# First layer's norm weights spread over the partitions by TensorE, and the last query tile taken before the triangular solve

## Chip, cores, metric

One NeuronCore of a Trainium2 chip runs the whole program. The metric is device microseconds from start to end of one execution; runs of the same kernel mostly agree within 0.3%.

## What is computed

A decoder trunk of four residual layers on 256 tokens of width 1024, in float32: pooling mixer, gated DeltaNet, latent attention, pooling mixer again, then a final norm.

```python
def rmsnorm(x, g):
    y = x * rsqrt(mean(x * x, axis=-1) + EPS)
    return y * g                              # g: one weight per column

for i in range(4):
    h = rmsnorm(x, norm_g[i])                 # norm_g: (4, 1024)
    x = x + mixer[i % 3](h)                   # each mixer: input projection ... output projection
return rmsnorm(x, final_g)

# DeltaNet (layer 1), per chunk and head: a lower triangular system
L = where(strict, k_beta @ k.T * decay, 0)
sol = triangular_solve(eye + L, [v_beta, k_beta * exp(g)])
```

## The kernel before

Tokens lie on the 128 partitions in two tiles, t = 0 and 1 (`xs[t]`). Each projection streams weights from HBM: `weights` (L97) loads a piece into a `raw` tile with a DMA from SyncE (SP), ScalarE (ACT) makes a rounded copy `whi` (L117), and VectorE (DVE), or for a few pieces GpSimd (POOL), makes the rest `wlo` (L119). Activations are split the same way (`split_out`, L196 and L201), and every product takes three TensorE matmuls (L127 to L129 where channels lie on partitions, L168 where tokens do).

**The order of the work is not written by hand.** The kernel is traced in program order, and a planner, told so in `build` (L1261), fixes ahead of time the order in which each engine issues, from its own estimate of how long things take. It also packs the tiles into SBUF: a tile may be given bytes that an earlier tile has left, and its first writer then waits for that tile's last reader. All engines issue strictly in the order fixed. Where the program wants an order kept, it says `later(ins)` (issue behind `ins` on the same engine).

**The start.** `load_x(0)` loads the first token tile. 24 transposes of the identity (`WARM`, L270) keep TensorE at work. `LayerIn(0)` then loads the norm weights: `gain_tile` (L273) spreads one row of 1024 floats over all partitions by two broadcasting DMAs on SP's queue, 256 KB in SBUF each, with the first weight piece between them. `start(0)` (L1218) computes the sum of squares (L210, ACT), the power -0.5 (L297, POOL, `xr`), the product of x, `xr` and gain (L304, DVE, `h`), turns h with TensorE (L324) and splits it into `hTh` and `hTl`, the operands of the first matmuls. Two weight pieces are split ahead of that, two more behind it (`E0`, `E1`). `load_x(1)` and `start(1)` do the same for the second token tile, queued behind the last of these pieces on ACT and DVE; there, half of each product is begun on POOL (`begin`, L292) and finished by ACT (L309).

**The solve.** In `gdn_layer` the steps run as `g0 k0 d a0 g1 k1 a1 s q0 v0 v1 v2 q1 V3 i c3 g2 u0 u1 g3` (L560). `s` is `substitution` (L714): the triangle's diagonal blocks go to HBM and come back as one tile `Lb`, then 31 steps on POOL follow, each a product `pr` that reads `Lb` (L728) and a subtraction into `Tb` (L732). `Tb` goes back over HBM (L735, then four DMAs L739) into `T`. `q0` and `q1` are the two halves of the queries (`channels`, L661): a convolution (L634 ACT, L637 DVE) into `cv`, SiLU on ACT into the tile `kqT` (L671), transposes on TensorE (L677) and products with the keys (L690). `v0` to `V3` are the values (L784 to L791, tile `vR`). `i` is `inverses` (L801): it transposes T (L811, DVE) and starts with products of T (L820, TensorE), both queued by `later` behind the last matmul and the last `wlo` of `V3`. `g2` is a gate whose matmuls have line L168. Tiles of all these, 4 KB a partition each, come from one pool (`big`, L70).

```python
    def channels(dst, c0, hf, which):          # L661
        banks = project(...)
        dst.append(big("kqT", 4, S))           # L665: the tile that is written by SiLU
    def substitution():                        # L714
        ...
        Lb = big("Lb", B, B)[:M * Q]           # L722
```

Of the kernel before, what the change touches and what calls it, by code (L numbers as in the profile page):

```python
# [8 lines left out]
F32 = mybir.dt.float32  # L9
# [7 lines left out]
P = 128  # L17
# [25 lines left out]
def trunk(ctx: ExitStack, tc: tile.TileContext, x, positions, norm_g, pool_w_in, pool_w_grp,  # L43
# [3 lines left out]
    nc = tc.nc  # L47
    PSUM = bass.MemoryType.PSUM

    WARM = 24  # L50
    FREE = 4
    EARLY = 6
    E0 = 2
# [200 lines left out]
    def load_x(t):  # L254
        for c in range(2):
            sl = slice(c * CW, (c + 1) * CW)
            nc.sync.dma_start(out=xs[t][:, sl], in_=x[0, t * P:(t + 1) * P, sl])

    load_x(0)
    neghalf = const.tile([P, 2], F32, name="neghalf")  # L260
    nc.gpsimd.memset(neghalf, -0.5)
    half = const.tile([P, 1], F32, name="half")
# [5 lines left out]
    nc.scalar.activation(warm, neghalf, AF.Silu)  # L268
    ps = bank(tps, "tp")
    for _ in range(WARM):  # L270
        nc.tensor.transpose(ps[:, :P], ident, ident)

    def gain_tile(row, between):  # L273
        g = gp.tile([P, D], F32, tag="gain", name="gain")
        for c in range(2):
            sl = slice(c * CW, (c + 1) * CW)
            nc.sync.dma_start(out=g[:, sl], in_=row[:, sl].to_broadcast([P, CW]))
            if c == 0 and between:
                between()
        return g  # L280

    class Normed:

        def __init__(self, row, between=None):
            self.g, self.early = gain_tile(row, between), {}

        def begin(self, t, a):
            sl = slice(a, a + CUT)  # L290
# [4 lines left out]
        def rest(self, t):  # L295
            r = small("xr", 1)
            mark["pool"] = nc.gpsimd.tensor_tensor(out=r, in0=ms[t], in1=neghalf[:, :1],  # L297
                                                   op=ALU.pow).ins
            hs = []
            for a in range(0, D, CW):  # L300
                h = wh.tile([P, CW], F32, tag="h", name="h")
                cut = CUT if (t, a) in self.early else 0
                sl = slice(a + cut, a + CW)
                nc.vector.scalar_tensor_tensor(out=h[:, cut:], in0=xs[t][:, sl], scalar=r[:, 0:1],  # L304
                                               in1=self.g[:, sl], op0=ALU.mult, op1=ALU.mult)
                hs.append(h)
                if not cut:
                    continue
                mark["rest"] = nc.scalar.activation(h[:, :CUT], self.early.pop((t, a)), AF.Copy,  # L309
                                                    scale=r[:, 0:1]).ins  # L310
            return hs

    class LayerIn(Normed):


        def __init__(self, i, between=None):
            super().__init__(norm_g[i:i + 1, :], between)
            self.hT = Split("hT", KD)

        def feed(self, t):  # L320
# [215 lines left out]
    def gdn_layer(i, j, hT):  # L536
# [121 lines left out]
        def power(o, a):  # L658
            nc.gpsimd.tensor_tensor(out=o, in0=a, in1=half, op=ALU.pow)

        def channels(dst, c0, hf, which):  # L661

            banks = project(cols_of(w_in, c0 + hf * CW), units(KD), hT, chan=True,
                            pool=() if which else (0, 4))
            dst.append(big("kqT", 4, S))  # L665
            for b in range(2):
                cv = [worka("cv", S) for _ in range(2)]
                conv(*[(banks[b][:, c * S:(c + 1) * S], (c0 + hf * CW) // P + 2 * b + c, cv[c])
                       for c in range(2)])
                for c in range(2):  # L670
                    nc.scalar.activation(dst[hf][:, 2 * b + c, :], cv[c], AF.Silu)  # L671
            for c in range(0, 4, 2):
                ps = bank(tps, "tp").rearrange("p (t a s) -> p t a s", a=2, t=NT)
                h = 4 * hf + c
                for a in range(2):
                    for t in range(NT):
                        nc.tensor.transpose(ps[:, t, a, :], dst[hf][:, c + a, t * P:(t + 1) * P],  # L677
                                            ident)
                sq = worka("sq", NT, 2, P)
                nc.scalar.activation(sq, ps, AF.Square)  # L680
                nc.vector.tensor_reduce(ssq[:, which, :, h:h + 2], sq, axis=AX.X, op=ALU.add)
                if which == 0:
                    nc.vector.tensor_copy(ktok[:, h:h + 2, :], ps[:, 0])
# [29 lines left out]

        def substitution():  # L714

            d_l = dram.tile([M * Q, B * B], F32, name="d_l")
            lv = d_l.rearrange("(t m d) (r c) -> t d r m c", t=NT, d=Q, r=B)
            for t in range(NT):
                for d in range(Q):
                    nc.sync.dma_start(out=lv[t, d],  # L720
                                      in_=LT[t][d * B:(d + 1) * B, :, d * B:(d + 1) * B])
            Lb = big("Lb", B, B)[:M * Q]  # L722
            nc.sync.dma_start(out=Lb, in_=d_l.rearrange("m (r c) -> m r c", r=B))
            pr = small("pr", 256, bufs=1)[:M * Q]
            for r in range(B - 1):
                n, c = B - 1 - r, r + 1
                pv = pr[:, :n * c].rearrange("m (a b) -> m a b", a=n)
                nc.gpsimd.tensor_tensor(out=pv, op=ALU.mult,  # L728
                                        in0=Lb[:, r, r + 1:, None].to_broadcast([M * Q, n, c]),
                                        in1=Tb[:, r:r + 1, :c].to_broadcast([M * Q, n, c]))  # L730
                tv = Tb[:, r + 1:, :c]
                mark["blocks"] = nc.gpsimd.tensor_tensor(out=tv, in0=tv, in1=pv,  # L732
                                                         op=ALU.subtract).ins
            d_t = dram.tile([M * Q, B * B], F32, name="d_t")
            nc.gpsimd.dma_start(out=d_t.rearrange("m (r c) -> m r c", r=B), in_=Tb)  # L735
            tv = d_t.rearrange("(m d) (r c) -> d r m c", d=Q, r=B)
            for d in range(Q):
                dd = slice(d * B, (d + 1) * B)
                nc.gpsimd.dma_start(out=Ts[dd, :, :, dd].rearrange("p t h c -> p (t h) c"),  # L739
                                    in_=tv[d])  # L740
            nc.vector.reciprocal(rki, rk)
            nc.vector.tensor_tensor(out=kds, in0=rk[:, 0, :], in1=DT[0][:, :, P - 1],
                                    op=ALU.mult)
            nc.vector.tensor_scalar(neG, eG[:, 1, :], -1.0, None, ALU.mult)
            nc.gpsimd.tensor_tensor(out=ktok, in0=ktok, op=ALU.mult,
                                    in1=kds[:, :, None].to_broadcast([P, H, P]))
# [470 lines left out]

    def start(t):  # L1218
        with later(*held_back["after"], *[mark[e] for e in ("act", "dve") if t]):
            for a in range(0, D, CW):  # L1220
                part_done(t, a, CW, apart=True)
            for a in range(0, D, CW):
                if t:
                    nxt.begin(t, a)
            nxt.feed(t)

    held_back["free"] = 100
    nxt = LayerIn(0, lambda: prefetch(0, (0,)))
    for k in range(1, E0):
        prefetch(k)  # L1230
    start(0)
# [40 lines left out]
```

## Time and profile before

| | |
|---|---|
| three runs | 859.98, 860.16, 857.79 us; median 859.98 |
| profiled execution | 860.12 us; its span 858.3 us (1.8 us lie outside) |
| TensorE (PE) busy | 836.9 us, 98% of the span |
| DVE, ACT, POOL busy | 69%, 57%, 18% |
| DMA | 140.4 MB, 164 GB/s over the span |

A row of the timeline gives start, duration, engine, line, operation, output<-inputs; in brackets how long that engine (PE matmuls, PEld weight loads) sat idle before it and what released it. Busy PE is not PE at its best pace: at half clock it is busy too.

### The profile page before, as it was taken

The numbers are of one execution on the slowest core, as the hardware profiler recorded it, in microseconds if no ns is written. First come the engines' busy times: TensorE is split into PE (matmuls) and PEld (weight loads), VectorE is DVE, ScalarE is ACT, GpSimd is POOL, SyncE is SP. The second block draws the span as 40 slices with busy tenths as digits, with TensorE's granted clock in tenths as the row PEclk, the third lists the DMA queues.
The fourth block names the chain that finished last, engine by engine and source line by source line (L and its number), as shares of the span: only waits on it lengthen the run. The fifth ranks groups of instructions, "written<-read, shape, count | busy, mean of one in ns | idle before, by whom it ended". The sixth has DMA issues, their size and how long they took to land.

```text
span 858.3 us, 16132 instructions
## 1 busy us (share of the span) xinstructions
PE 836.9 (98%) x5967; PEld 778.9 (91%) x5967; DVE 594.2 (69%) x1140; ACT 490.2 (57%) x1007; POOL 155.2 (18%) x295
## 2 busy tenths in 40 slices
PE   6999999999999989999999999999999999999996
PEld 5999998988999988788979998999989989999986
DVE  4689866556988976355577659678767668867852
ACT  5566564467855744355465654566555475555642
POOL 4000000233237980022212002000000210000012
PEclk8999999999999999899999999999999999999999
DMA  6766666646655554123547676743552546556551
GB/s 196 245 190 185 179 194 198 194 138 198 193 141 168 171 149 131 66 67 106 173 139 217 198 171 172 195 127 97 172 163 82 175 148 209 182 179 196 190 201 50
DMA packets 109239, 140.42 MB, mean 164 GB/s; under 512 B 21228, under 2 KB 51112, under 8 KB 109160
## 3 DMA queue, kind: packets, MB, share of 16 engines
q1 hardware_dynamic: 106800, 137.65, 53.1%
q0 software_dynamic: 528, 1.58, 0.7%
q8 instruction: 47, 0.77, 0.4%
q10 hardware_dynamic: 1832, 0.16, 0.2%
q14 instruction: 32, 0.26, 0.1%
HBM read 137.79 MB, written 1.58 MB: 162 GB/s over the span
## 4 chain that ended last, share of the span: by engine, by line
PE 82%; POOL 7%; DVE 5%; DMA 3%; issue 2%; ACT 1%; SPq 0%; POOLq 0%; ACTq 0%; DVEq 0%
PE acc L168 33%; PE acc L128 11%; PE acc L127 11%; PE acc L129 11%; POOL Tb L732 3%; POOL pr L728 2%; PE aux L127 2%; PE aux L128 2%; PE aux L129 2%; DVE wlo L119 1%; DMA gain<-in_norm_g_dram 1%; DVE cv L637 1%; DVE h L304 1%; PE aux L861 1%; DMA Gb<-d_g 1%
## 5 line engine op out<-in xcount | busy, mean ns | idle before, releaser
L119 DVE TENSOR_TENSOR wlo<-raw,whi 128x512 fp32r<-128x512 f32 (+1 forms) x493 | 342.5, 717 | 162.6 <-ACT whi L117 155.4
L117 ACT CAST whi<-raw 128x512 fp32r<-128x512 f32 (+1 forms) x508 | 301.8, 617 | 256.7 <-PE acc L168 100.4
L127 PE MATMUL acc<-hTh,whi 128*128 128x256 f32 x832 | 234.3, 282 | 1.2 <-DVE vc L637 1.2
L128 PE MATMUL acc<-hTl,whi 128*128 128x256 f32 x832 | 235.0, 283 | 0.0
L129 PE MATMUL acc<-hTh,wlo 128*128 128x256 f32 x832 | 233.8, 281 | 0.0
L127 PEld LDWEIGHTS acc<-hTh,whi 128*128 128x128 f32 x832 | 156.9, 189 | 1.8 <-DVE vc L637 1.4
L128 PEld LDWEIGHTS acc<-hTl,whi 128*128 128x128 f32 x832 | 156.9, 189 | 0.4
L129 PEld LDWEIGHTS acc<-hTh,wlo 128*128 128x128 f32 x832 | 156.8, 189 | 0.2
L168 PE MATMUL acc<-wlo,yTh 128*128 128x256 f32 (+1 forms) x384 | 116.5, 319 | 0.0
L168 PE MATMUL acc<-whi,yTh 128*128 128x256 f32 (+1 forms) x384 | 116.4, 323 | 0.0
L168 PE MATMUL acc<-whi,yTl 128*128 128x256 f32 (+1 forms) x384 | 92.7, 322 | 0.0
L168 PEld LDWEIGHTS acc<-wlo,yTh 128*128 128x128 f32 x384 | 72.1, 188 | 5.1
L168 PEld LDWEIGHTS acc<-whi,yTh 128*128 128x128 f32 x384 | 71.7, 188 | 5.2
L168 PEld LDWEIGHTS acc<-whi,yTl 128*128 128x128 f32 x384 | 63.2, 188 | 5.5
L292 POOL TENSOR_TENSOR hg<-x,gain 128x256 f32<-128x256 f32 x18 | 14.9, 834 | 259.1 <-DVE x L354 257.4
L168 PE MATMUL acc<-wlo,hTh 128*128 128x512 f32 (+1 forms) x144 | 56.3, 396 | 0.4 <-DVE wlo L119 0.2
L168 PE MATMUL acc<-whi,hTh 128*128 128x512 f32 (+1 forms) x144 | 55.6, 394 | 0.7 <-ACT hTh L196 0.7
L168 PE MATMUL acc<-whi,hTl 128*128 128x512 f32 (+1 forms) x144 | 45.7, 389 | 0.0
L435 POOL COPY win<-u 128x4 f32<-128x4 f32 x8 | 2.8, 355 | 177.2 <-ACT u L429 177.2
L168 PEld LDWEIGHTS acc<-whi,hTh 128*128 128x128 f32 x144 | 27.5, 191 | 6.8 <-ACT hTh L196 1.7
L168 PEld LDWEIGHTS acc<-wlo,hTh 128*128 128x128 f32 x144 | 27.3, 190 | 6.8 <-DVE wlo L119 1.7
L168 PEld LDWEIGHTS acc<-whi,hTl 128*128 128x128 f32 x144 | 26.8, 190 | 5.5
(339 smaller groups left out, 1444.5 us busy)
## 6 DMA issues: line engine op xcount, KB each, us to landing
raw<-in_pool_w_in_dram SPq DMA_DIRECT2D x60, 512.0 KB, 4.5
raw<-in_gdn_w_in_dram SPq DMA_DIRECT2D x48, 512.0 KB, 3.9
raw<-in_pool_w_out_dram SPq DMA_DIRECT2D x32, 512.0 KB, 4.2
raw<-in_mla_w_in_dram SPq DMA_DIRECT2D x24, 512.0 KB, 4.6
raw<-in_mla_w_uq_dram SPq DMA_DIRECT2D x36, 256.0 KB, 3.4
raw<-in_pool_w_grp_dram SPq DMA_DIRECT2D x16, 512.0 KB, 4.1
raw<-in_gdn_w_out_dram SPq DMA_DIRECT2D x16, 512.0 KB, 3.7
raw<-in_mla_w_ukv_dram SPq DMA_DIRECT2D x32, 256.0 KB, 3.3
```

The costliest lines, as they stand in the source:

```text
L117: a = nc.scalar.copy(hi, v)
L119: b = e.tensor_tensor(out=lo, in0=v, in1=hi.bitcast(F32), op=ALU.subtract)
L127: nc.tensor.matmul(o, lhsT=lhs[0], rhs=rhs[0], start=start, stop=False)
L128: nc.tensor.matmul(o, lhsT=lhs[0], rhs=rhs[1], start=False, stop=False)
L129: return nc.tensor.matmul(o, lhsT=lhs[1], rhs=rhs[0], start=False, stop=stop)
L168: nc.tensor.matmul(o, lhsT=act(k, t * P, P)[x], rhs=parts[j][z][:, sl], start=k == first and x == z == 0, stop=k == last and x == 1)
L292: nc.gpsimd.tensor_tensor(out=self.early[t, a], in0=xs[t][:, sl], in1=self.g[:, sl], op=ALU.mult)
L304: nc.vector.scalar_tensor_tensor(out=h[:, cut:], in0=xs[t][:, sl], scalar=r[:, 0:1], in1=self.g[:, sl], op0=ALU.mult, op1=ALU.mult)
L637: nc.vector.scalar_tensor_tensor(out=o[:, d:], in0=ps[:, :S - d], scalar=tp(3 - d, c), in1=o[:, d:], op0=ALU.mult, op1=ALU.add)
L728: nc.gpsimd.tensor_tensor(out=pv, op=ALU.mult, in0=Lb[:, r, r + 1:, None].to_broadcast([M * Q, n, c]), in1=Tb[:, r:r + 1, :c].to_broadcast ...
L732: mark["blocks"] = nc.gpsimd.tensor_tensor(out=tv, in0=tv, in1=pv, op=ALU.subtract).ins
L861: nc.tensor.matmul(ps[:, c], lhsT=U[0][:, h, :], rhs=vR[h // 2][:, 0, c * DV:(c + 1) * DV], start=True, stop=True)
```

## The change

The first layer's norm weights are no longer spread by DMA. One row (4 KB) is loaded to one partition by a DMA on ACT's queue, ahead of everything else; two matmuls with a row of ones as the stationary operand write it to all partitions of two PSUM banks; they are pinned behind the warm-up transposes, of which there are 6 in place of 24. For the first token tile, DVE reads the weights from PSUM. For the second, ACT first copies both banks into an SBUF tile, since POOL reads them there. SP's queue loses the two broadcasts. The later layers load their norm weights as before.

In the DeltaNet layer, the tile of the second half of the queries is allocated at the head of `substitution`, with a one-column memset on POOL as its first write, so that its life overlaps that of `Lb` and it can't be given the same bytes. `channels` then uses that tile.

```diff
-    WARM = 24
+    WARM = 6
...
+    grow0 = const.tile([1, D], F32, name="grow0")
+    nc.scalar.dma_start(out=grow0, in_=norm_g[0:1, :])
     load_x(0)
+    ones = const.tile([1, P], F32, name="ones")
+    nc.gpsimd.memset(ones, 1.0)
...
     for _ in range(WARM):
-        nc.tensor.transpose(ps[:, :P], ident, ident)
+        tc.keep_in_program_order(nc.tensor.transpose(ps[:, :P], ident, ident))
+    gains0 = []
+    for c in range(2):
+        ps = bank(aux, "aux")
+        tc.keep_in_program_order(nc.tensor.matmul(ps, lhsT=ones, rhs=grow0[:, c * CW:(c + 1) * CW],
+                                                  start=True, stop=True))
+        gains0.append(ps)
...
-                                               in1=self.g[:, sl], op0=ALU.mult, op1=ALU.mult)
+                                               in1=self.g[:, sl] if self.g is not None else gains0[a // CW],
+                                               op0=ALU.mult, op1=ALU.mult)
...
+        taken = {}
+
+        def take(hf):
+
+            taken[hf] = big("kqT", 4, S)
+            nc.gpsimd.memset(taken[hf][:, 0, :1], 0.0)
...
-            dst.append(big("kqT", 4, S))
+            dst.append(taken[hf] if which and hf in taken else big("kqT", 4, S))
...
         def substitution():
 
+            take(1)
...
     def start(t):
         with later(*held_back["after"], *[mark[e] for e in ("act", "dve") if t]):
+            if t:
+                nxt.g = gp.tile([P, D], F32, tag="gain", name="gain")
+                for c in range(2):
+                    nc.scalar.copy(nxt.g[:, c * CW:(c + 1) * CW], gains0[c])
...
-    nxt = LayerIn(0, lambda: prefetch(0, (0,)))
+    nxt = LayerIn(0)
+    prefetch(0, (0,))
```

## Rows read from the trace of the kernel before

**Rows 1.** The page, part 4: engines' shares of the chain that ended last.
```profile
PE 82%; POOL 7%; DVE 5%; DMA 3%; issue 2%; ACT 1%; SPq 0%; POOLq 0%; ACTq 0%; DVEq 0%
```

**Rows 2.** PE's waits over the whole span: total us, times, longest us.
```profile
PE tp L324 <- DVE h L304: 4.4, 2, 2.4
PE tp L677 <- ACT kqT L671: 3.0, 3, 2.4
```

**Rows 3.** The timeline of the start, first token tile.
```profile
3.44 0.63 ACT L210 ACTIVATE junk<-x 128x512 f32<-128x512 f32 x1 [1.15 <-DMA x<-in_x_dram]
...
5.42 0.57 POOL L297 TENSOR_TENSOR xr<-ms,neghalf 128x1 f32<-128x1 f32 x1
...
7.83 0.75 DVE L304 SCALAR_TENSOR_TENSOR h<-x,xr,gain 128x512 f32<-128x512 f32 x1 [7.83 <-DMA gain<-in_norm_g_dram]
...
8.64 1.11 PE L324 MATMUL tp<-ident,h 128*128 128x128 f32 x4 [2.41 <-DVE h L304]
...
9.87 1.26 POOL L119 TENSOR_TENSOR wlo<-raw,whi 128x512 fp32r<-128x512 f32 x1 [3.88 <-ACT whi L117]
10.16 1.52 DVE L304 SCALAR_TENSOR_TENSOR h<-x,xr,gain 128x512 f32<-128x512 f32 x1 [1.57 <-DMA gain<-in_norm_g_dram]
...
11.74 1.11 PE L324 MATMUL tp<-ident,h 128*128 128x128 f32 x4 [1.99 <-DVE h L304]
```

**Rows 4.** The same timeline, second token tile and the weights between.
```profile
12.50 0.78 PE L168 MATMUL acc<-whi,hTh 128*128 128x512 f32 x1
...
12.81 1.43 POOL L292 TENSOR_TENSOR hg<-x,gain 128x256 f32<-128x256 f32 x2 [1.67 <-DMA x<-in_x_dram]
...
13.37 1.14 ACT L117 CAST whi<-raw 128x512 fp32r<-128x512 f32 x2
...
16.38 0.40 PE L168 MATMUL acc<-whi,hTl 128*128 128x512 f32 x1
...
17.48 1.09 PE L324 MATMUL tp<-ident,h 128*128 128x128 f32 x8 [0.70 <-ACT h L309]
```

**Rows 5.** Stages of the start: busy us by engine, PEclk granted, DMA share, GB/s.
```profile
6.00:7.00 1.00, 0.23 (x3) 0.00 (x0) 0.00 (x0) 0.00 (x0) 0.00 (x0) 1.00 0.73 205
...
9.00:10.00 1.00, 0.75 (x4) 0.35 (x2) 0.00 (x0) 0.62 (x1) 0.13 (x1) 0.50 1.03 395
```

**Rows 6.** DMA issues up to 30 us: count, KB each, median us to landing.
```profile
rows<-in_pool_scale_dram ACTq DMA_DIRECT2D x2, 8.0 KB, 4.6
```

**Rows 7.** Groups by line up to 60 us: busy, mean ns, idle before.
```profile
L429 ACT COPY u<-acc 128x512 f32<-128x512 f32 x2 | 1.2, 588 | 0.4 <-issue 0.4
```

**Rows 8.** The timeline around the end of the solve.
```profile
299.02 0.85 ACT L791 ACTIVATE vR<-tp,rki 128x256 f32<-128x256 f32 x2
...
305.29 0.42 ACT L671 ACTIVATE kqT<-cv 128x256 f32<-128x256 f32 x1 [3.46 <-POOL pr L728]
...
305.76 0.69 PE L677 MATMUL tp<-ident,kqT 128*128 128x128 f32 x2 [2.41 <-ACT kqT L671]
...
306.25 1.12 DVE L119 TENSOR_TENSOR wlo<-raw,whi 128x512 fp32r<-128x512 f32 x1 [2.25 <-ACT whi L117]
```

**Rows 9.** Stages after that wait, columns as in group 5.
```profile
306.00:308.00 2.00, 2.00 (x11) 2.00 (x11) 1.75 (x3) 1.71 (x5) 1.86 (x3) 0.50 0.32 124
308.00:310.00 2.00, 2.00 (x16) 2.00 (x16) 1.97 (x5) 1.07 (x3) 2.00 (x3) 0.82 0.62 131
318.00:348.00 30.00, 30.00 (x185) 25.14 (x184) 19.17 (x33) 12.66 (x24) 3.19 (x4) 1.00 0.44 141
```

**Rows 10.** The chain that ended last, 298 to 325 us: start, us, what.
```profile
310.47 0.45 PE aux L690 x4
...
315.38 3.03 PE acc L168 x13
```

**Rows 11.** The way of T: POOL's timeline, DVE's timeline, and line L820's instructions.
```profile
311.48 2.68 POOL L739 DMA_DIRECT2D T<-d_t  x4
...
318.75 2.37 DVE L811 STREAM_TRANSPOSE U<-T 128x1024 f32<-128x1024 f32 x2 [1.91 <-DMA T<-d_t]
...
L820 PE MATMUL aux<-T,LT x32: 275/275/283, 318.3 to 330.3; 128*128 128x64 f32 x32
```

More of the change, by code (lines that the diff above doesn't have):

```diff
@@ L270, in trunk, with gain_tile @@
     for _ in range(WARM):
-        nc.tensor.transpose(ps[:, :P], ident, ident)
-    def gain_tile(row, between):
+        tc.keep_in_program_order(nc.tensor.transpose(ps[:, :P], ident, ident))
[5 more added lines that the diff above has]
+        gains0.append(ps)
+    def gain_tile(row):
         g = gp.tile([P, D], F32, tag="gain", name="gain")
@@ L277, in gain_tile, with __init__ @@
             nc.sync.dma_start(out=g[:, sl], in_=row[:, sl].to_broadcast([P, CW]))
-            if c == 0 and between:
-                between()
         return g
     class Normed:
-        def __init__(self, row, between=None):
-            self.g, self.early = gain_tile(row, between), {}
+        def __init__(self, row):
+            self.g, self.early = None if row is None else gain_tile(row), {}
         def begin(self, t, a):
@@ L313, in trunk, with __init__ @@
     class LayerIn(Normed):
-        def __init__(self, i, between=None):
-            super().__init__(norm_g[i:i + 1, :], between)
+        def __init__(self, i):
+            super().__init__(norm_g[i:i + 1, :] if i else None)
             self.hT = Split("hT", KD)
```

## The prediction

> **What bounds the kernel now.** First the chain that ended last: TensorE holds 82% of it, POOL 7% and DMA 3% [rows 1]. So time is won only where TensorE stands still or runs at half clock, or where a POOL or DMA stretch holds it. Then TensorE's own waits, over the whole span [rows 2]: two of the largest are the ones that this change touches, 4.4 us for h of the first layer and 3.0 us for the queries' tile `kqT`. The timeline shows what lies behind each. At the start, `xr` is ready at 5.42 + 0.57 = 5.99, but the first h starts at 7.83 and the second at 10.16, both released by the broadcasting DMA of the norm weights [rows 3]. At the solve, ACT stands 3.46 us before its first write of `kqT`, released by POOL's L728, the product that reads `Lb`: the new tile has the old one's bytes. TensorE stands 2.41 us for it and DVE 2.25 us, since the weight casts are queued behind ACT's waiting instruction [rows 8]. After that TensorE has a clock of 0.50 for 2 us and a mean of 0.82 for two more [rows 9]: 2 x 0.50 + 2 x 0.18 = 1.4 us of work lost. That 1.4 is my price for one fall of the clock.
>
> **The start, step by step.** *The row.* The gain row's DMA goes first on ACT's queue, at about 0.8, where SP's first issue is now. Nothing in the trace is quite like it. The first half of x, 64 times as large and issued at the same moment, is in use at 3.44 [rows 3]; rows of 8 KB on the same queue took 4.6 us, with other DMAs under way [rows 6]. So it lands between 3.4 and 5.4; I take 3.4, the row of the same stretch. *The matmuls.* Two float32 products of 128 columns, four instructions, take 0.45 us at full clock [rows 10], so 512 columns take 0.9 and both 1.8: done at 5.2, behind r at 5.99, hence free; from 5.4 and at half clock they would end at 9.0. The 18 warm-ups removed lay before any real work and cost nothing. *h.* From 5.99: 0.75, then 0.75 more. The second now takes 1.52, beside a POOL product of two SBUF tiles (9.87 to 11.13) [rows 3]. The transposes of each are 1.11 at the clock of now [rows 3], so they run 6.8 to 7.9 and 7.9 to 9.0, against 12.85: 3.8 us earlier. The first weights also come earlier: 512 KB less at the 205 to 395 GB/s of these stages [rows 5] is 2.5 to 1.3 us.
>
> The Trainium skill says (GPSIMD Engine Reference, 8. Key points) that POOL shares SBUF interfaces with VectorE and that they contend when a VectorE instruction has two SBUF inputs. The trace agrees, 1.52 against 0.75 us. By that rule the new h, with one input from PSUM, escapes it; without the rule the second h would end at 8.3 and the step would give 3.4 instead of 3.8.
>
> *The second token tile* sets when TensorE runs on without a break. Its sums of squares are queued on ACT behind two casts that now end at 14.51 [rows 4]; these move by 3.8 to 10.7. The change puts two copies from PSUM ahead of or among the sums, 0.588 each [rows 7], 1.2 together. x's second tile is there at 12.81 [rows 4], after the change 1.3 to 2.5 earlier, 10.3 to 11.5, so it is no later than ACT by more than 0.8, and then the copies lie in that wait. The gain at the second transposes (17.48 now [rows 4]) is 3.8 - 1.2 = 2.6; the ends are 3.8 (copies hidden) and 0.8 (the row late, 2.0, less 1.2). *The gap.* The twelve matmuls of the first token tile end at 16.78 now and would end at 13.0; the transposes follow at 14.9, so TensorE stands 1.9 us where it stands 0.7 [rows 4]. Idle stretches of 2.41 us at the start and at the solve were followed by half clock [rows 3, 5, 8, 9]. 1.9 is shorter, and a fifth weight piece may fill part of it: I take half the price, 0.7, ends 0 and 1.4. **Start: 2.6 - 0.7 = 1.9 us faster**, ends 3.8 faster and 0.6 slower.
>
> **The solve, step by step.** The wait of `kqT` on `Lb` goes: 2.41 idle + 1.4 clock = 3.8 us for TensorE, or at least the 2.25 that DVE wins if DVE's convolutions and casts set the pace. The memset on POOL is one column and stands before the 31 steps; bytes are free there if the tile gets ones that have not been used for long, so nothing. *What is late next* is T. It depends on POOL alone: the 31 steps end where they did, POOL goes on without a pause to the four DMAs L739 at 311.48 to 314.16, and DVE stood 1.91 us for their landing until 318.75 [rows 11]. TensorE's first use, L820, runs at 318.3 without a wait [rows 11], which is no accident of slack: TensorE came there late by exactly the stall before. If it comes 2.3 to 3.8 us earlier, it waits there that long, and DVE waits with it, with the casts behind L811.
>
> Would the planner put other work in front? It has 13 matmuls L168 of the gate there already, 3.03 us [rows 10]. In its order, ACT's write of `kqT` stands ahead of a weight cast that could have run [rows 8]: a planner that counted on the 3.46 us would have cast first. So its estimate of POOL is too fast, the stall is not in its plan, and without the stall its plan stays what it is. T stays at 318.3, TensorE starts again there, and since the new gap of 2.3 to 3.8 is nearest to the 2.41 that brought half clock, I add 1.4; the end 0 stands for no fall. From 318 to 348 TensorE has hardly a break to absorb it [rows 9]. The Trainium skill (TensorE: Matmul & The Clock Gate, Part 1) holds that idleness throttles TensorE to half and activity releases it; the 0.50 after the wait agrees [rows 9]; by it the end 0 is unlikely. **Solve: 1.4 us slower**, ends 3.8 faster and 1.4 slower.
>
> **Sum.** 860.1 (the profiled execution, 0.1 above the median of 859.98) - 1.9 + 1.4 = **859.6**. Own range, with the start's ends and 0 to 1.4 for the solve: 856.5 to 862.
>
> **Rivals.**
> *1. The plan adapts.* L820 is put some 16 matmuls further back (3.8 us at 3.03 / 13 = 0.23), as filler is there until the end of the gates. For it: the plan is made anew for the new program. Against: see above. Then 860.1 - 1.9 - 3.8 = 854.4.
> *2. The place passes on (slower).* The tile taken early occupies bytes that another tile had, and a later one gets `Lb`'s. Between s and q1, six tiles are allocated; the last, the third values' `vR`, is written by ACT from 299.02 [rows 8]. If it is the one, ACT stands from there until 305.29: 6.3 us in place of 3.46, 2.8 more, with the convolutions and casts of the queries behind it, and TensorE passes L820 at 321. That is also how the change would not do what it says: it decides from the point where the wait is 3.46 + 1.9 = 5.4 us, that is, where the waiting write is queued before 299.9. With 1.9 from the start 861.0, with nothing from it 862.9. For it: bytes were short enough for one reuse. Against: inverses' tiles are later and may take them at no cost.
> *3. The row is late.* At 5.4 us, TensorE cold: the second half of h's weights at 9.0, its transposes at 10.9, 2.0 earlier than now; less 1.2 for the copies and 0.7 for the gap nothing remains: 860.1 - 0.1 + 1.4 = 861.4.
>
> **How the numbers follow.** A run of this kernel can tell 0.3%, 2.6 us, from no change. Forecast 0.50, of which 0.09 lies below 857.4 (no fall of the clock in either gap) and 0.03 above 862.6; rival 1 0.26, all faster; rival 2 0.13, of which 0.08 is slower by over 2.6, since the start then gives little; rival 3 0.11, of which 0.05. Faster 0.09 + 0.26 = 0.35, slower 0.03 + 0.08 + 0.05 = 0.16, the same 0.49. The range takes in rival 1 with its start between 1.3 and 2.6, so from 853.7, and rivals 2 and 3 to 862.7.
>
> **What the changed profile would show.** Right: no DMA of gain in the first 15 us; first h at about 6.0, second transposes from 7.9; the second token tile's transposes near 14.9, with a gap of about 1.9 before them; ACT's first `kqT` of the second half with no wait on L728; and in its place TensorE waiting at L820, DVE at L811 for `T<-d_t` by more than 1.91. Wrong, at the start: a gap on DVE until a matmul lands, or the copies ahead of sums that were ready. Wrong, at the solve: TensorE without a wait at L820 and more matmuls L168 before it (rival 1), or ACT waiting for L728 with another tile (rival 2).

## The result: slower, by the new wait at the inverses

| | median | runs, lowest to highest | profiled execution, its span |
|---|---|---|---|
| before | 858.86 us | 10, 857.79 to 860.65 | 860.12, 858.3 |
| after | 862.60 us | 10, 860.38 to 865.58 | 862.61, 860.9 |

The ratio is 1.0036, 95% interval 1.0021 to 1.0051: 3.1 us slower by the ratio (1.8 to 4.4), 3.7 by the medians. The time lies inside the range of the forecast, 853.7 to 862.7, but at its slow end, where the forecast had no change.

TensorE's waits over the whole span of the changed kernel (total us, times, longest; [rows 2] are those of before) tell most of it:

```profile
PE aux L838 <- DMA T<-d_t: 6.6, 1, 6.6
PE tp L694 <- ACT kqT L688: 2.9, 2, 2.5
...
PE tp L334 <- DVE h L313: 0.6, 1, 0.6
```

L838 is the old L820, the first product with the inverses; L694 is L677, L334 is L324. The wait for h has shrunk from 4.4 to 0.6. The one for the queries' tile behind the solve is gone: what stands here at L694 is another, at 260, behind weights that came late. A new wait of 6.6 us stands at the inverses.

**The start**, as in [rows 3, 4] (start, us, engine, line, form, idle before and its releaser):

```profile
3.57 3.78 PE L280 MATMUL aux<-grow,ones 1*128 1x512 f32 x4
6.01 0.75 DVE L313 SCALAR_TENSOR_TENSOR h<-x,xr,aux 128x512 f32<-128x512 f32 x1 [6.01 <-POOL xr L306]
7.10 1.17 DVE L119 TENSOR_TENSOR wlo<-raw,whi 128x512 fp32r<-128x512 f32 x1 [0.35 <-ACT whi L117]
8.20 0.73 DVE L313 SCALAR_TENSOR_TENSOR h<-x,xr,aux 128x512 f32<-128x512 f32 x1
8.99 1.11 PE L334 MATMUL tp<-ident,h 128*128 128x128 f32 x4 [0.60 <-DVE h L313]
9.76 0.77 PE L168 MATMUL acc<-whi,hTh 128*128 128x512 f32 x1
17.03 0.66 PE L334 MATMUL tp<-ident,h 128*128 128x128 f32 x4 [0.25 <-ACT h L319]
```

The first h starts at 6.01, released by r and not by a transfer. The two products that spread the row take 3.78 us. VectorE puts a weight's low part ahead of the second h, and the second transposes start at 8.99. TensorE stands hardly at all before the second token tile: the first weights' products fill the time.

**The end of the solve**, beside [rows 8, 11]:

```profile
299.61 0.47 ACT L688 ACTIVATE kqT<-cv 128x256 f32<-128x256 f32 x1
312.49 2.68 POOL L757 DMA_DIRECT2D T<-d_t  x4
316.75 0.62 ACT L117 CAST whi<-raw 128x512 fp32r<-128x512 f32 x1 [7.30 <-DMA raw<-in_gdn_w_in_dram]
318.90 3.65 PE L838 MATMUL aux<-T,LT 128*128 128x64 f32 x16 [6.59 <-DMA T<-d_t]
319.37 2.37 DVE L829 STREAM_TRANSPOSE U<-T 128x1024 f32<-128x1024 f32 x2 [9.50 <-DMA T<-d_t]
```

ACT's first write of the last queries comes at 299.61, without a wait (305.29 after 3.46 before). The four transfers of the inverses are issued 1.0 us later than in [rows 11], and TensorE and VectorE stand 6.59 and 9.50 us for their landing. Nothing fills the time on TensorE, since it issues strictly in its order and the products with the inverses are next in it. The weights for the products behind them were late as well: ACT stands 7.30 us for a raw weight, and SP's load of it waited 9.9 us for a weight's low part on POOL, L119, which is queued there behind the solve's work.

The stretches around that wait (us, then the busy time of TensorE, weight load, VectorE, ACT, POOL, the granted clock, DMA share, GB/s; [rows 9] before):

```profile
312.00:319.00 7.00, 0.41 (x3) 0.13 (x1) 0.00 (x0) 1.88 (x5) 6.81 (x12) 0.88 0.61 187
319.00:326.00 7.00, 7.00 (x25) 6.23 (x26) 6.63 (x12) 0.60 (x1) 1.83 (x3) 0.50 0.39 108
326.00:328.00 2.00, 2.00 (x7) 1.56 (x6) 1.64 (x5) 0.91 (x2) 0.00 (x0) 0.62 0.40 155
```

TensorE is at the lower of its two levels, 0.50, for the 7 us behind the wait, and at a mean of 0.62 for two more: 7 x 0.50 + 2 x 0.38 = 4.3 us of work lost. The kernel before lost 1.4 behind its 2.41.

### The profile page after: what moved, and what is told of

It reads as the page before. It is cut to its first block, busy times and chain, and to the rows that moved or that the text cites. A ratio compares the mean times of both kernels' runs of the same rounds, so it can differ in the third digit from the quotient of the medians.

```text
span 860.9 us, 16103 instructions
## 1 busy us (share of the span) xinstructions
PE 838.7 (97%) x5953; PEld 777.8 (90%) x5953; DVE 592.1 (69%) x1140; ACT 492.5 (57%) x1009; POOL 158.0 (18%) x297
## 4 chain that ended last, share of the span: by engine, by line
PE 85%; POOL 7%; DVE 2%; DMA 2%; ACT 2%; issue 1%; SPq 0%; POOLq 0%; ACTq 0%
PE acc L168 34%; PE acc L128 12%; PE acc L127 12%; PE acc L129 12%; POOL pr L746 3%; POOL Tb L750 2%; PE aux L127 2%; PE aux L128 2%; PE aux L129 2%; DVE h L313 1%; DMA T<-d_t 1%; PE aux L838 1%; PE tp L1202 1%; DMA Lb<-d_l 1%; PE aux L879 1%
## 5 line engine op out<-in xcount | busy, mean ns | idle before, releaser
L119 DVE TENSOR_TENSOR wlo<-raw,whi 128x512 fp32r<-128x512 f32 (+1 forms) x493 | 340.8, 713 | 165.3 <-ACT whi L117 162.1
L168 PE MATMUL acc<-whi,yTh 128*128 128x256 f32 (+1 forms) x384 | 116.5, 323 | 0.0
L168 PE MATMUL acc<-wlo,yTh 128*128 128x256 f32 (+1 forms) x384 | 116.4, 319 | 0.0
L168 PE MATMUL acc<-whi,yTl 128*128 128x256 f32 (+1 forms) x384 | 92.6, 321 | 0.0
L168 PEld LDWEIGHTS acc<-wlo,yTh 128*128 128x128 f32 x384 | 72.2, 188 | 5.1
L168 PEld LDWEIGHTS acc<-whi,yTh 128*128 128x128 f32 x384 | 71.7, 188 | 5.2
L168 PEld LDWEIGHTS acc<-whi,yTl 128*128 128x128 f32 x384 | 63.2, 188 | 5.6
L168 PE MATMUL acc<-wlo,hTh 128*128 128x512 f32 (+1 forms) x144 | 58.2, 407 | 0.6 <-DVE wlo L119 0.3
L168 PE MATMUL acc<-whi,hTh 128*128 128x512 f32 (+1 forms) x144 | 56.7, 400 | 0.7 <-ACT hTh L196 0.7
L168 PE MATMUL acc<-whi,hTl 128*128 128x512 f32 (+1 forms) x144 | 46.7, 397 | 0.0
L168 PEld LDWEIGHTS acc<-wlo,hTh 128*128 128x128 f32 x144 | 28.2, 196 | 7.8 <-DVE wlo L119 2.6
L168 PEld LDWEIGHTS acc<-whi,hTh 128*128 128x128 f32 x144 | 28.1, 195 | 6.7 <-ACT hTh L196 1.4
L168 PEld LDWEIGHTS acc<-whi,hTl 128*128 128x128 f32 x144 | 27.5, 195 | 5.6
```

The costliest lines, as they stand in the source:

```text
L119: b = e.tensor_tensor(out=lo, in0=v, in1=hi.bitcast(F32), op=ALU.subtract)
L168: nc.tensor.matmul(o, lhsT=act(k, t * P, P)[x], rhs=parts[j][z][:, sl], start=k == first and x == z == 0, stop=k == last and x == 1)
```

## The experiments

Ratios are against the kernel before, run on the same chip beside it, with a 95% interval. The theory that the first of them test: the way from the solve to the inverses (the stores of the triangle's diagonal blocks to HBM, called the band from here on, their load back as `Lb`, 31 steps on POOL, a store, four loads) sets the end of this stretch, so that a freed wait ahead of it only moves.

### The two parts apart

Start alone: the changed kernel without

```
-            take(1)
```

> The start's part alone: the row of gain spread by TensorE, the six warm-up transposes, the copies; the last queries' tile takes its place where it did before. Theory (T's way sets the end of the solve, and the freed wait on the queries' tile only moves the stall to the inverses): TensorE waits for the queries' silu and the band as before (about 3 us before the transposes of the queries), the inverses wait not at all or under 1 us, and the 2.4 us by which the changed kernel was ahead at the first band stay to the end, so about 2.4 us less than the kernel before (ratio 0.997, 0.995 to 0.999). Rival (the start's part itself is what costs, by its copies, by the half clock of its gain products or by a plan that comes out otherwise): no gain or slower, ratio 1.000 to 1.004.

Solve alone: the kernel before with `take`, its call, and

```
-            dst.append(big("kqT", 4, S))
+            dst.append(taken[hf] if which and hf in taken else big("kqT", 4, S))
```

> The solve's part alone: the kernel before with the last queries' tile taken ahead of the solve, the start unchanged. Theory: the wait on the queries' tile is gone, the inverses wait 3 to 6 us instead, TensorE is at half clock for some 7 us behind that wait in place of 2 to 3 us, and the run is 2 to 5 us longer than before (ratio 1.002 to 1.006). The steps of the solve on POOL take over 45 us if VectorE's casts beside them are what lengthens them, and 44.6 us as before if it was the start's shift that lengthened them. Rival (the start is to blame): same as before or faster by up to 3.8 us (ratio 0.9955 to 1.000).

| | median | ratio |
|---|---|---|
| start alone | 858.57 us | 0.9988 (0.9972 to 1.0003) |
| solve alone | 863.33 us | 1.0034 (1.0018 to 1.0050) |

TensorE's waits around the solve, start alone and then solve alone (timeline):

```profile
304.89 0.44 PE L694 MATMUL tp<-ident,kqT 128*128 128x128 f32 x2 [2.41 <-ACT kqT L688]
```

```profile
318.53 3.64 PE L828 MATMUL aux<-T,LT 128*128 128x64 f32 x16 [6.63 <-DMA T<-d_t]
```

So the solve's part is what costs: 2.9 us by its ratio, 1.5 to 4.3, with the same 6.6 us of wait. The start's part does not cost, but gives about 1 us, and its interval reaches zero. The two together make 1.9, inside the interval of the whole change (1.8 to 4.4). The start's 1 us is less than the 2.4 expected. Two things in the traces bear on it. First, the start of one execution is no fixed number. The solve-alone kernel has the start of the kernel before, in the same order on TensorE, and there the second transposes came at 10.22 and those of the second token tile at 16.16, against 11.74 and 17.48 [rows 3, 4]. The execution that the forecast rested on began 1.3 us late. The band's stores begin at 249.0 in the solve-alone execution and at 248.3 in the changed kernel: a lead of 0.7 us, where the late execution (250.7) shows 2.4. And since the solve alone waits 6.63 us too, with nothing of the start's change in it, most of the 2.4 within that wait comes from the late execution. Second, in the start-alone trace the band's stores begin 2.1 us earlier than before but the first step on POOL only 0.9 (rows of that line: form, count, shortest/median/longest ns, first and last start; before, then start alone):

```profile
L720 SPq DMA_DIRECT2D d_l<-LT x8: 340/449/640, 250.7 to 254.0; - x8
L728 POOL TENSOR_TENSOR pr<-Lb,Tb x31: 232/564/966, 261.0 to 305.0; 64x31 f32<-64x31 f32 x2, 64x60 f32<-64x60 f32 x2, 64x87 f32<-64x87 f32 x2, 64x112 f32<-64x112 f32 x2
```

```profile
L737 SPq DMA_DIRECT2D d_l<-LT x8: 340/448/1513, 248.6 to 253.3; - x8
L745 POOL TENSOR_TENSOR pr<-Lb,Tb x31: 233/566/968, 260.1 to 304.2; 64x31 f32<-64x31 f32 x2, 64x60 f32<-64x60 f32 x2, 64x87 f32<-64x87 f32 x2, 64x112 f32<-64x112 f32 x2
```

The eight issues take 4.7 us in place of 3.3, and the slowest of these stores lands after 3.5 us in place of 2.2. From 261 on the end of the stretch hangs on POOL, in the kernel before as well (its queries wait for POOL's last reading of `Lb`), so of a lead ahead of the solve only what reaches POOL survives.

### The clock behind the wait

```
+                ps = bank(tps, "tp")
+                for _ in range(56):
+                    tc.keep_in_program_order(nc.tensor.transpose(ps[:, :P], ident, ident))
                 with later(mark["strip"], mark["dve"]):
                     inverses()
```

> The changed kernel with 56 more transposes of the identity between the last row products before the inverses and the inverses; nothing uses them. They only fill TensorE's wait: the inverses start when they did, but TensorE was busy meanwhile. Theory (the half clock behind the wait costs about 4 us of its own): the stretch behind the inverses is at full clock, and the run is 3 to 4 us shorter than the changed kernel, about level with the kernel before (ratio to before 0.999 to 1.001). Rival 1 (the clock behind the wait costs little, the lateness of the inverses is all): same as the changed kernel (ratio 1.0036). Rival 2 (the added transposes are themselves late, at half clock or held up by their bank): longer than the changed kernel by up to 6 us.

862.63 us, ratio 1.0031 (1.0017 to 1.0045): level with the changed kernel, as rival 1 has it. Yet the trace does not bear rival 1 out:

```profile
318.58 1.97 PE L838 MATMUL aux<-T,LT 128*128 128x64 f32 x16 [1.63 <-DMA T<-d_t]
```

```profile
319.00:326.00 7.00, 6.97 (x37) 5.57 (x36) 6.63 (x13) 0.00 (x0) 0.40 (x2) 1.00 0.09 35
```

The clock is 1.00 behind the inverses, and the 16 products take 1.97 us in place of 3.65. But the planner made its order anew: between the first product with the inverses and the first with the state (L915, tile `st`, the step behind the inverses) there are now 98 row products L168, in the changed kernel 84. 13 of the 14 had stood ahead of the inverses. At 0.23 each [rows 10] the 14 are 3.3 us, done in the same 46 us. By this count the half clock had cost some 3 us, near the 4.3 that the windows give, and the experiment gave them away again by its order. That is counted from the trace and not shown by the total, on which the experiment is inconclusive.

### The inverses earlier

```
-                nc.gpsimd.dma_start(out=Ts[dd, :, :, dd].rearrange("p t h c -> p (t h) c"),
-                                    in_=tv[d])
+                mark["blocks"] = nc.gpsimd.dma_start(
+                    out=Ts[dd, :, :, dd].rearrange("p t h c -> p (t h) c"), in_=tv[d]).ins
```

`mark["blocks"]` is what POOL's work for the last queries is queued behind; so far it was the solve's last step.

> The changed kernel with POOL's work for the last queries queued behind the four transfers of the inverses to memory instead of between or ahead of them. Theory (the way of the inverses from the solve to TensorE sets the end): the inverses reach TensorE 1 to 2 us sooner, its wait for them is shorter by as much, and the run is 1 to 2 us shorter than the changed kernel (ratio to before 1.001 to 1.003), unless the queries that now come later are then waited for. Rival (the inverses are not what sets the end): no change against the changed kernel (1.0036).

858.42 us, ratio 0.9985 (0.9970 to 0.9999): 4.4 us shorter than the changed kernel by the two ratios, more than the 1 to 2 expected. POOL and TensorE:

```profile
305.75 0.64 POOL L753 DMA_DIRECT2D d_t<-Tb  x1 [0.29 <-POOL Tb L750]
309.07 2.01 POOL L757 DMA_DIRECT2D T<-d_t  x3 [2.68 <-DMA d_t<-Tb]
312.94 2.35 PE L838 MATMUL aux<-T,LT 128*128 128x64 f32 x16 [2.68 <-DMA T<-d_t]
```

The products with the inverses start at 312.94 in place of 318.90. Of the 6.0 us, 3.4 come from the issue (309.07 for 312.49), and only part of these from the queue's order: the last step on POOL ends at 305.46 in place of 307.32, 1.9 earlier, and from there to the issue it takes 3.6 us in place of 5.2. Three of the four transfers go ahead of POOL's work for the queries; the fourth, issued at 312.31, stands behind its first product. Most of the rest is the landing: 2.4 us for each of the four in place of 4.5 to 5.5. Raw weights move less at that time, which was not tested by itself as the cause: the DMA share around the landing is 0.36 (309 to 315), in the changed kernel 0.61 (312 to 319), and in the experiment before it, where the same four took 6.1 to 6.7, 0.77.

Is it the inverses' lateness that costs, or is POOL's new order a gain by itself? The same edit with the start's part alone (`take(1)` left out):

> The start's part alone, with the inverses' four transfers ahead of POOL's work for the last queries, and the queries' tile where it was before. Theory (as long as TensorE waits at the queries' tile, the inverses come in time and are not what is waited for): the inverses land some 3 us sooner and nothing comes of it, the run is level with the start's part alone (ratio to before 0.998 to 0.9995). Rival (the order on POOL's queue gives its gain by itself, whatever stands ahead): 3 to 4 us shorter than the start's part alone (ratio to before 0.994 to 0.996).

858.63 us, ratio 0.9987 (0.9972 to 1.0002): level with the start alone at 0.9988, where the inverses also were in time. TensorE's waits from 290 to 330:

```profile
PE tp L694 <- ACT kqT L688: 3.0, 1, 3.0
PE acc L127 <- DVE vc L647: 1.0, 1, 1.0
```

It waits for the queries' tile as before and for the inverses not at all. The theory holds on both sides: inverses that come earlier, by the order on POOL's queue and by shorter steps together, are worth 4 us where they are waited for, and nothing where the queries' tile is waited for ahead of them. It also prices the change itself: with the inverses ahead, taking the tile early (858.42) is worth no more than not taking it (858.63), a wait of 2.7 us at the inverses in place of one of 3.0 at the tile.

### Why the steps on POOL got longer

From the first step to the end of the last, the solve took 44.6 us before and in both kernels with the tile in its old place; 47.1 with the solve's part alone and 47.6 in the changed kernel. With the busy wait and with the inverses earlier, where the tile is early too, it took 45.5 and 45.7, so the tile's place alone does not make the 3 us. POOL's and VectorE's rows of the changed kernel, of the same moment:

```profile
265.46 0.50 POOL L750 TENSOR_TENSOR Tb<-Tb,pr 64x156 f32<-64x156 f32 x1
266.04 1.59 POOL L746 TENSOR_TENSOR pr<-Lb,Tb 64x175 f32<-64x175 f32 x1
```

```profile
265.21 0.87 DVE L647 SCALAR_TENSOR_TENSOR vc<-acc,tap,vc 128x255 f32<-128x255 f32 x2
266.00 1.28 DVE L119 TENSOR_TENSOR wlo<-raw,whi 128x512 fp32r<-128x512 f32 x2
```

A step of 64x175 that starts with a pair of casts (two inputs from SBUF) ends just after them, 1.59 us; beside the convolutions, which read PSUM, a step of 64x156 takes 0.50. In the experiment above (inverses earlier), where no cast is on VectorE at that moment, the same 64x175 takes 0.48. To test the size, the cast was given no input in the five stages beside the solve:

```
+                if mark.get("single") and e is nc.vector:
+                    b = e.memset(lo.bitcast(F32), 0.0)
+                else:
+                    b = e.tensor_tensor(out=lo, in0=v, in1=hi.bitcast(F32), op=ALU.subtract)
```

> The changed kernel with VectorE's subtraction that makes the low part of a weight (two inputs) replaced by a fill with zeros (no input) in the five stages beside the solve's steps on POOL; the low parts of those weights are left out of the sum. Theory A (POOL's steps are long because VectorE's work with two inputs runs against them): the 31 steps, 47.6 us in the changed kernel and 44.6 us in the one before, take under 42 us, the inverses' wait of 6.6 us shrinks by the same, and the run is 3 to 6 us shorter. Theory B (the steps' length comes from elsewhere, POOL's own accesses): the steps take 44 to 48 us still and the run stays within 1 us of the changed kernel, but for what the shorter casts give.

A single profiled execution, 850.52 us. The steps took 40.8 us, from 253.93 to 294.72, and TensorE waited 0.5 us for the inverses. Theory A holds: 6.8 us of the 47.6 go with VectorE's casts, as far as one execution shows it. The run itself is 12 us shorter, more than theory A's 3 to 6, since these casts are also shorter for VectorE and the solve already began 5.8 us earlier; what share each has is not told apart. The Trainium skill (GPSIMD Engine Reference, 8. Key points) has the rule, that POOL and VectorE share SBUF interfaces and contend when a VectorE instruction has two SBUF inputs; the rows above and the 6.8 us agree with it. Over all the other runs the length of the steps goes with how many of these casts VectorE does beside them: 24 or 25 (21.8 to 22.1 us) in the three kernels with 44.6, 26 or 27 (23.1 to 23.7 us) in the four with 45.2 to 45.7, 28 to 31 (23.8 to 24.8 us) in the six with 47.1 to 48.2. Within a group it is a matter of which steps coincide.

### Filling the wait

Third gate's weights cast without POOL, and its 48 row products ahead of the inverses in TensorE's order:

```
-                            pool=((0, 4), (7,), (3, 7), (7,))[vi])
+                            pool=((0, 4), (7,), (), (7,))[vi])
-        order = "g0 k0 d a0 g1 k1 a1 s q0 v0 v1 v2 q1 V3 i c3 g2 u0 u1 g3".split()
+        order = "g0 k0 d a0 g1 k1 a1 s q0 v0 v1 v2 q1 V3 c3 g2 i u0 u1 g3".split()
-                with later(mark["strip"], mark["dve"]):
+                with later(rowmark["row"]):
```

> The changed kernel with the third gate's weights cast without POOL and its 48 row products put ahead of the inverses in TensorE's order. The inverses come no sooner; TensorE has work of its own in the wait. Theory (the wait of 6.6 us and the half clock behind it, some 3 us, are what is lost at the inverses): the wait is under 1 us, the stretch behind is at full clock, and the run is 5 to 9 us shorter than the changed kernel (854 to 858 us, ratio to before 0.994 to 0.999). Rival (the inverses' lateness itself is the bound, since VectorE's work behind them is the longer way): level with the changed kernel or 2 us shorter at most (ratio 1.001 to 1.004).

With the inverses' transfers first as well:

> Both the queue's order of the fourth experiment (the inverses' four transfers ahead of POOL's work for the last queries) and the third gate's row products ahead of the inverses. Theory: in the fourth experiment 2.7 us of wait and 1.7 us of half clock were left at the inverses; with the gate's products there, about 4 us go again: 854 to 855 us, ratio to before 0.994 to 0.996. Rival (what is left after the fourth experiment is on another way, or the gate's casts on VectorE cost what the wait gave): 857 to 860 us, ratio 0.998 to 1.001.

The first: 861.25 us, ratio 1.0024 (1.0007 to 1.0041). The second: 858.58 us, 0.9990 (0.9978 to 1.0002). Both theories failed on the total. In the second the wait at the inverses was gone, and the first product with the state came at 357.49, in place of 360.72 with the transfers alone. Two stretches gave it back; with the filler, and then with the transfers alone:

```profile
326.00:350.00 24.00, 21.09 (x150) 18.85 (x150) 8.01 (x13) 4.67 (x8) 0.00 (x0) 0.82 0.32 99
680.00:700.00 20.00, 16.86 (x105) 14.50 (x106) 13.01 (x23) 14.05 (x30) 5.50 (x10) 1.00 0.50 155
```

```profile
326.00:350.00 24.00, 24.00 (x154) 19.73 (x153) 9.66 (x15) 11.11 (x22) 1.30 (x1) 1.00 0.37 126
680.00:700.00 20.00, 19.62 (x131) 17.31 (x130) 11.81 (x22) 13.29 (x29) 4.92 (x10) 1.00 0.40 131
```

From 326 to 350 TensorE now stands in the inverses' own chain (it waits in turn for X and for the copies of T, tiles of that chain, 2.9 us), where the gate's products had lain between; the clock falls to 0.82 there. From 660 to 700, in the last layers, it stands 3.2 us more than with the transfers alone. The order of work had come out differently there too.

Two variants keep one or two of these casts on POOL, so that the late order stays:

> The seventh experiment with one of the third gate's casts left on POOL (the last unit's, behind the inverses' transfers), so that the order of all engines in the later layers is that of the fourth experiment. Theory (in the seventh experiment the wait at the inverses was gone and the 3 to 4 us it gave were lost again in a later layer whose order had come out otherwise): the wait at the inverses is under 1 us, the first product with the state comes 2 to 4 us sooner than in the fourth experiment, and here it stays: 854 to 856 us, ratio to before 0.994 to 0.997. Rival (the wait only moves on, to this one cast or to VectorE behind the inverses): 857 to 860 us, ratio 0.998 to 1.001.

> As the ninth, but the third gate has no cast on POOL and the fourth has two. Theory: as the ninth, 854 to 856 us, ratio to before 0.994 to 0.997, with no wait of TensorE on POOL's cast in the third gate. Rival: as the ninth, 857 to 860 us.

862.84 us, ratio 1.0066 (1.0051 to 1.0080), and 863.22 us, 1.0067 (1.0051 to 1.0083): slower than all others, the wait had moved on to the values' transposes. The first of them:

```profile
SPq L104 <- POOL rq L782: 11.1, 1, 11.1
...
325.39 1.18 PE L806 MATMUL tp<-ident,vc 128*128 128x128 f32 x8 [2.39 <-ACT vc L802]
```

SP, whose waits from 290 to 330 the first row is from, stands 11.1 us before it can load the next raw weight. The row names a small POOL operation of the queries, but the chain that ended last shows the load under way before that one ends at 319.00, and just behind a weight's low part on POOL, which reads a raw tile (start, us, what):

```profile
317.15 1.69 POOL wlo L119
318.84 0.03 POOL rq L782
318.87 3.85 DMA raw<-in_gdn_w_in_dram
```

So by the times it is the low part that SP waits for, and it stands on POOL behind the queries' work. ACT stands 7.39 us for that weight, until 322.80, and the chain runs from there over its low part on VectorE and ACT's copies for the values to TensorE. One low part left on POOL holds a row of engines. In the second variant, TensorE's wait at the values' transposes is 4.9 us.

Two more have no cast of the third gate on POOL and another count of warm-up transposes, 10 and 24, which gives another order in the last layers:

> The seventh experiment (inverses' transfers first, the third gate's 48 products ahead of the inverses, no cast of that gate on POOL) with ten warm-up transposes instead of six. Nothing of it is near the inverses, but the planner's order of the last two layers comes out as in the ninth experiment instead of the seventh's. Theory (the seventh lost its 3 to 4 us there, to loads of weights that came later in that order): TensorE has no wait of over 0.5 us between 640 and 720, the lead at the first product with the state stays, and the run takes 853 to 856 us (ratio to before 0.993 to 0.997). Rival (the loss in the late layers follows from arriving there earlier, or from the gate's casts, whatever the order): 857 to 860 us, ratio 0.998 to 1.001.

> The same with the 24 warm-up transposes of the kernel before; the order of the last two layers is that of the fourth experiment, instruction for instruction. Theory for the late layers: as the eleventh experiment, no wait of over 0.5 us between 640 and 720. For the start: the warm-ups end later, so that the two products that spread the row of gain start up to 2 us later but at a higher clock; between 1 us shorter and 2 us longer than the eleventh, 853 to 857 us (ratio to before 0.993 to 0.998). Rival: the loss in the late layers is there again, 857 to 861 us.

858.86 us, ratio 0.9984 (0.9969 to 0.9999), and 859.37 us, 0.9993 (0.9978 to 1.0008). The loss in the last layers is gone as the theory has it (between 640 and 740 no wait over 0.5 us), so that loss goes with the order there and not with the filler. An arrival 3 us early as its cause is not ruled out: these two come to the first product with the state at 360.74 and 359.15, the kernel with the loss at 357.49. The total is no better. Of the 10-transposes kernel:

```profile
326.00:350.00 24.00, 21.88 (x151) 19.25 (x150) 10.80 (x16) 7.29 (x14) 0.00 (x0) 0.89 0.34 110
350.00:366.00 16.00, 15.13 (x67) 12.66 (x67) 4.63 (x10) 5.72 (x15) 0.00 (x0) 0.75 0.01 2
```

The first product with the state comes at 360.74, as with the transfers alone. Between 300 and 320 TensorE never stands; from 326 to 366 it stands 3.0 us and loses 24 x 0.11 + 16 x 0.25 = 6.6 to the clock, where with the transfers alone it stands 0.9 and loses 3.4. In these kernels the gate's products fill the wait for the inverses or the pauses behind them, not both. No version that computes everything beat the kernel before by more than 0.2%: the transfers ahead, at 0.9985, and this one, at 0.9984, are the best, and both beat the changed kernel by some 4 us.

## Why the prediction was wrong

**Right: the start's mechanism, and most of its times.** The row was there by 3.57 (forecast 3.4), h at 6.01 (6.0), the second transposes at 8.99 (7.9). Mis-sized were the two products, 3.78 us in place of 1.8: each took about twice my figure, which I had read off at full clock. It cost 0.5 at the first transposes (7.28 for 6.8) and nothing at the second, since the second h was held up by a weight's low part on VectorE, 1.17 us (7.10 to 8.27), until after the products were done; the forecast had nothing between the two. The gap of 1.9 before the second token tile did not come, nor a fall of the clock for it: seven more of the first tile's products (19 in place of 12) ran before it. The transposes started at 17.03 rather than 14.9, split in two, with products between them. The lead at the band's stores, 2.4 us against the forecast 1.9, looks right but is luck: the base was one execution that began late, and against the other start on record the lead is 0.7 (above). It also shrank on the way to POOL. At the end the start was worth 1.0 us, 2.4 faster to 0.3 slower by its interval.

**Right: the place of `kqT`.** ACT's first write of the last queries does not wait, and no other tile took over the wait on `Lb` (rival 2).

**Right: what is late next, and that the plan stays.** TensorE waits at the inverses, with exactly 13 row products ahead of them as before. Rival 1 was wrong where it said that filler is there: the weights for it were held up on POOL and SP.

**Failed: "T stays at 318.3".** The step said that T depends on POOL alone and that the 31 steps end where they did. It depends on POOL, but POOL's steps depend on VectorE. The first step started 1.2 us earlier and the last ended 1.7 later (307.32 for 305.58): more of VectorE's casts ran beside them, 30 for 24. Of the 2.9 us, 1.9 came from 301 on, in the last ten of the 62 instructions of the steps: VectorE no longer stood its 2.25 us there, and five casts ran beside these ten in place of one. The other 1 us, net of small gains between, came in the first 8 us of the steps (the 64x175 above is one of them), long before that stall. The busy wait and the inverses-earlier kernel, with the early tile too, lost 0.7 and 1.0 in the last ten and hardly anything in the first. So about 1 us goes with the freed stall; why the casts fell so badly on the other steps stays open. T came at 318.9. A move of 0.6 is small, but the sum also took the start's 1.9 as won at the end, that is, T as coming earlier by it. It came no earlier: a lead of TensorE ahead of a fixed T turns into wait.

**Failed: the size of the solve's term, 1.4.** Measured by itself, that term is 2.9 us slower (1.5 to 4.3). The forecast was 2.3 to 3.8 of wait and 1.4 for one fall of the clock. It was 6.59, about the 3.8 freed, the 2.4 between the two executions ahead of the solve and the 0.6 by which T came later. I had not carried my own 1.9 from the start into the wait, and my base came late to it. And the price of a fall is not a constant: 1.4 us behind 2.41 of idleness, 4.3 behind 6.59. Together 10.9 us are lost at the inverses where 3.8 were lost at the tile. That is 7.1, less 2.4 from the start 4.7; the first product with the state comes 3.0 later (364.9 for 361.9). The difference is a stretch of low clock just ahead of that product, which cost less after the change (before, then after):

```profile
350.00:361.90 11.90, 10.92 (x52) 9.04 (x52) 2.23 (x5) 3.46 (x10) 0.00 (x0) 0.71 0.13 44
```

```profile
350.00:364.90 14.90, 13.38 (x87) 10.91 (x85) 4.49 (x8) 5.48 (x13) 0.00 (x0) 0.89 0.19 68
```

The loss there is 11.9 x 0.29 = 3.4 us before and 14.9 x 0.11 = 1.6 after, 1.8 less, and 4.7 - 1.8 = 2.9. TensorE stands 1.5 us from 328 to that product in both.

**Half right: the Trainium skill's two rules.** The one on two SBUF inputs was cited for the second h alone; it bears on the solve's steps too (6.8 of 47.6 us, above), where I didn't look. The one on the clock (TensorE: Matmul & The Clock Gate, Part 1, idleness throttles TensorE to half and activity releases it) agrees with the 0.50 of 319 to 326, but what a wait costs had to be read from a row of its own length.

**The chances.** 0.16 for slower by over 0.3%, all in rivals 2 and 3 and the upper tail; what came was the forecast's own mechanism at its slow end and past it, which had 0.03. The forecast's own range, 856.5 to 862, is 856.3 to 862.1 by its own terms.

## What to carry to other kernels

Before a wait is taken away, follow the next producer that the engine will meet back to its own engine, and add to the new wait all that the same change wins ahead of it: here the freed time ended there, and with it the lead that TensorE had. A producer on POOL is not fixed while VectorE gets more to do beside it. And where the filler for a wait is the same work that hides the pauses behind it, moving it won nothing here.

## What the runs showed of the hardware

- A POOL step beside VectorE's casts: 0.48 us alone and 1.59 us with two casts (64x175), and it ends with them. In sum 6.8 of 47.6 us, in a single execution without the casts' input.
- The stretch at the lower clock, 0.50, grew with the wait: some 2.7 us of it behind 2.41 ([rows 9]) and some 8.5 behind 6.59 (rows above), with the means at 0.82 and 0.62 split into the two levels.
- In the start of the changed kernel the granted clock reads 1.00 throughout, yet TensorE's products there come at two paces, 0.43 us apart at first and 0.23 apart from 13.9 on. The granted clock of the first stretch is no safe guide to TensorE's pace there.

```profile
12.00:13.00 1.00, 1.00 (x4) 0.77 (x3) 0.65 (x2) 1.00 (x3) 0.67 (x1) 1.00 0.63 232
```

```profile
12.46 0.63 PE L168 MATMUL acc<-whi,hTh 128*128 128x512 f32 x1
12.89 0.63 PE L168 MATMUL acc<-wlo,hTh 128*128 128x512 f32 x1
...
13.87 0.39 PE L168 MATMUL acc<-wlo,hTh 128*128 128x512 f32 x1
14.10 0.39 PE L168 MATMUL acc<-whi,hTl 128*128 128x512 f32 x1
```

- Four loads of the inverses landed in 2.4 us each with a DMA share of 0.36 in that stretch (309 to 315, inverses earlier), and in 6.1 to 6.7 with 0.77 (312 to 319, busy wait). That the share is the cause was not tested by itself.
